# The write of the router weights, issued on ScalarE's DMA queue instead of SyncE's

## The chip, the core and the metric

The kernel runs on one core of a Trainium2 chip. The metric is the device time of one execution in microseconds; the kernel before took 3912.41 us, the median of three runs (3896.12 to 3922.23).

The names of the engines in the profile are PE (TensorE's matmuls), PEld (TensorE's weight loads), DVE (VectorE), ACT (ScalarE), POOL (GpSimd) and SP (SyncE, which here only issues DMAs). A "q" behind a name (SPq, ACTq) means the engine's sequencer, which waits, branches and issues DMAs.

## What is computed

The reference is one layer of a hybrid encoder on 1024 prompt tokens and 8 x 16 sample tokens, 1152 tokens in all, with width 1024: a mixer sublayer (banded attention beside a gated linear recurrence) and a PEER sublayer with 8 retrieval heads over 128 x 128 experts of one neuron each. The change lies on the way from the heads' choices to the weights of the experts:

```python
def peer_tokens(xt, wq, keys1, keys2, expert_u, expert_v):
    q = (xt @ wq).reshape(t, PEER_HEADS, 2, HALF_KEY)
    s1 = jnp.einsum('thd,hnd->thn', q[:, :, 0], keys1)
    s2 = jnp.einsum('thd,hnd->thn', q[:, :, 1], keys2)
    v1, i1 = lax.top_k(s1, TOPK_HALF)
    v2, i2 = lax.top_k(s2, TOPK_HALF)
    ...
    top_s, pos = lax.top_k(cand_s, TOPK)
    e_idx = jnp.take_along_axis(cand_i, pos, axis=-1)
    g = jax.nn.softmax(top_s, axis=-1)
    act = jax.nn.gelu(jnp.einsum('thkd,td->thk', expert_u[e_idx], xt))
    return jnp.einsum('thk,thkd->td', (g * act), expert_v[e_idx])
```

Each token has 8 x 16 chosen experts with a weight g each. As a matrix over all 16384 experts, g is nearly empty.

## The kernel before

The 1152 tokens are nine blocks of 128, in three groups of three. The mixer and the router run group by group. The experts are then computed in two ways. Four blocks (`GATHER`) fetch the chosen rows of `peer_u` and `peer_v` by indirect DMA on GpSimd's queue, and VectorE multiplies them (lines L915, L942, L963); this goes on beside everything else from about 700 us to the end. Five blocks (`DENSE`) are computed against all experts on TensorE at the end, from about 2060 us on, and need g as a full matrix `G_d` in DRAM, 128 x 128 experts by 640 tokens.

`build_g` makes that matrix, 32 tokens at a time, so 4 times a block and 20 times in all. One part of 8 tokens makes one-hot tiles on VectorE, 16 matmuls into two PSUM tiles `pg` (`products`, L1013 and L1014), and two ScalarE copies from `pg` into `st` (L1016). `st` holds 32 tokens, 128 partitions x 128 x 32 words, and its pool has one buffer, so the first L1016 of the next 32 tokens has to wait until the write of the last 32 has landed. The write is the line that changes, L1018: 2 MB from `st` to `G_d` in 8192 pieces of 256 bytes (64 words).

These parts are not a stage of their own. They stand in a list, `fill`, that `tick` empties a part at a time between the steps of the next group's mixer and router (L395 to L730), so the 20 writes fall between 980 and 2042 us: eight of them while the second group is in its attention, its output projections and its query projections, twelve while the third is. The instructions are then put in order, engine by engine, by a scheduler when the kernel is built; that order is fixed and every engine works through its own in order.

Before the change all weight loads and the write stand on one queue, SP's: `raw` (L149, a weight tile of 512 KB), `lo` (L159, the stored low part of a weight, 512 KB, read back instead of computed again), and smaller ones. ScalarE turns `raw` into `hi` (L158), and each projection is three matmuls a step (L170 to L172) with `hi` and `lo`. ScalarE's own queue carries other writes: keys and values (L484), router scores `s_d` (L730), and the rows of the residual and the normed tokens (L700, L708).

A built program counts the landing of its DMAs on eight semaphores, which the DMAs of both hardware queues take in turn: the DMA that is eighth after another takes the same one, and its issue waits until that other one has landed. With 8 semaphores and 20 writes, some of the DMAs that wait for a `G_d` write in this way are on ScalarE's queue.

Of the kernel before, what the change touches and what calls it, by code (L numbers as in the profile page):

```python
# [59 lines left out]
GCH = 2  # L60
# [10 lines left out]
def kernel(ctx, tc, a):  # L71
    nc = tc.nc
# [679 lines left out]
    def make_tables(b):  # L752
        if b in pending:
            pending.pop(b)()

    def table_parts(tab):
        h = tab.bitcast(F16)
        return h[:, 0:128], h[:, 128:256], tab[:, 128:192].bitcast(BF16), h[:, 384:512], h[:, 512:640]
# [213 lines left out]
    G_d = dr_p.tile([128, 128 // GCH, NCH, GCH, 32], F32, name="G_d")  # L972

    def build_g(gp, b):

        n0 = 4 * DENSE.index(b)
        st = {}

        def part(c, tb):
            def go():  # L980
                if c == 0 and tb == 0:
                    make_tables(b)
                    st["t"] = gp["st"].tile([128, 320], F32, name="tab")
                    nc.sync.dma_start(st["t"], tab_d[b])
                if tb == 0:
                    st["s"] = gp["st"].tile([128, 128, 32], F32, name="st")
                i1, i2, pw, hi, lo = table_parts(st["t"])
                sg = st["s"]
                t = c * 32 + tb * OH_T

                def row(x):
                    return x[:, t:t + OH_T].rearrange("p (g t) -> p g t", t=2).unsqueeze(2).to_broadcast(
                        [128, OH_T // 2, 128, 2])

                ow = gp["oh"].tile([128, OH_T // 2, 128, 2], BF16, name="ow")
                oh = gp["oh"].tile([128, OH_T // 2, 128, 2], F16, name="oh1")
                ol = gp["oh"].tile([128, OH_T // 2, 128, 2], F16, name="oh2")
                V.tensor_tensor(ow, gp["iota"], row(i2), op=ALU.is_equal)
                V.tensor_tensor(ow, ow, row(pw), op=ALU.mult)
                V.tensor_tensor(oh, gp["iota"], row(i1), op=ALU.is_equal)  # L1000
                V.tensor_tensor(ol, oh, row(lo), op=ALU.mult)
                V.tensor_tensor(oh, oh, row(hi), op=ALU.mult)
                later.append(lambda: products(c, tb, ow, oh, ol, sg))
                if len(later) > 1:
                    later.popleft()()
            return go

        def products(c, tb, ow, oh, ol, sg):
            for j0 in range(0, OH_T, 4):
                pg = ps_p.tile([128, 4, 128], F32, name="pg", tag="pp")  # L1010
                for j in range(4):
                    g, e = divmod(j0 + j, 2)
                    T.matmul(pg[:, j, :], ow[:, g, :, e], oh[:, g, :, e], start=True, stop=False)  # L1013
                    T.matmul(pg[:, j, :], ow[:, g, :, e], ol[:, g, :, e], start=False, stop=True)  # L1014
                t = tb * OH_T + j0
                S.activation(sg[:, :, t:t + 4].rearrange("p i t -> p t i"), pg, ACTF.Copy, scale=2.0 ** -13)  # L1016
            if tb == 32 // OH_T - 1:
                nc.sync.dma_start(G_d[:, :, n0 + c], sg.rearrange("p (a i) t -> p a i t", i=GCH))  # L1018

        later = deque()  # L1020
        return [part(c, tb) for c in range(4) for tb in range(32 // OH_T)] + [lambda: later.popleft()()]
# [290 lines left out]
```

## Time and profile before

| | |
|---|---|
| three runs | 3896.12, 3912.41, 3922.23 us |
| the profiled execution | 3894.32 us, of it 3892.5 us span |
| mean granted TensorE clock | 0.968 of full speed |
| TensorE busy | 3629.8 us, 93% of the span |
| VectorE, ScalarE, GpSimd busy | 78%, 42%, 37% |

The profile is of one execution, 18 us faster than the median of the runs. An engine's busy time leaves out what its sequencer does: waits and the issue of DMAs. The granted clock is a share of TensorE's full speed, 2.4 GHz; 0.5 is its lower level, 1.2 GHz. "idle before <- X" behind an instruction says how long its engine had nothing to run and what ended that.

### The profile page before, as it was taken

The numbers are of one execution on the slowest core, as the hardware profiler recorded it, in microseconds if no ns is written. First come the engines' busy times: TensorE is split into PE (matmuls) and PEld (weight loads), VectorE is DVE, ScalarE is ACT, GpSimd is POOL, SyncE is SP. The second block draws the span as 40 slices with busy tenths as digits, with TensorE's granted clock in tenths as the row PEclk, the third lists the DMA queues.
The fourth block names the chain that finished last, engine by engine and source line by source line (L and its number), as shares of the span: only waits on it lengthen the run. The fifth ranks groups of instructions, "written<-read, shape, count | busy, mean of one in ns | idle before, by whom it ended". The sixth has DMA issues, their size and how long they took to land.

```text
span 3892.5 us, 59562 instructions
## 1 busy us (share of the span) xinstructions
PE 3629.8 (93%) x21775; PEld 3258.9 (84%) x21775; DVE 3049.4 (78%) x6332; ACT 1624.7 (42%) x2699; POOL 1429.2 (37%) x1094
## 2 busy tenths in 40 slices
PE   8998899899988889988788989999999999999998
PEld 7877799877778887777778878999999999999997
DVE  8433357968766588987669999998888998888997
ACT  7554346656644664666443222222222222222222
POOL 0000000123212012322210666665675665775662
PEclk9999999999999999999889999999999999999999
DMA  7778887888999889899996999898998998998995
GB/s 256 252 247 300 287 295 276 301 315 281 284 358 349 300 299 315 298 290 284 334 337 216 345 326 342 320 347 332 359 339 310 346 347 326 336 349 324 342 343 206
DMA packets 558423, 1208.05 MB, mean 310 GB/s; under 512 B 205361, under 2 KB 281521, under 8 KB 558129
## 3 DMA queue, kind: packets, MB, share of 16 engines
q1 hardware_dynamic: 380560, 638.23, 47.3%
q0 software_dynamic: 147456, 536.94, 38.4%
q10 hardware_dynamic: 30112, 29.09, 2.2%
q8 instruction: 170, 2.79, 0.3%
q14 instruction: 125, 1.02, 0.1%
HBM read 1066.15 MB, written 137.94 MB: 309 GB/s over the span
## 4 chain that ended last, share of the span: by engine, by line
PE 61%; DVE 13%; DMA 10%; ACT 6%; issue 3%; POOL 0%; ACTq 0%; SPq 0%; DVEq 0%; POOLq 0%
PE S L1085 19%; PE pp L170 12%; PE pp L171 12%; PE pp L172 12%; DMA G_d<-st 4%; DVE row L942 3%; PE S L529 2%; ACT st L1016 2%; DMA row<-peer_u,ei 1%; PE pt L458 1%; PE pp L543 1%; ACT hi L158 1%; DVE x L963 1%; DMA lo<-lo_w_in 1%; DVE lo L137 1%
## 5 line engine op out<-in xcount | busy, mean ns | idle before, releaser
L915 POOL DMA_INDIRECT row<-peer_u,ei x512 | 715.2, 1397 | 1172.0 <-DVE row L942 508.6
L915 POOL DMA_INDIRECT row<-peer_v,ei x512 | 687.8, 1343 | 793.4 <-DVE x L963 543.0
L963 DVE SCALAR_TENSOR_TENSOR x<-row,q,x 128x1024 f32<-128x1024 f32 x512 | 655.0, 1279 | 21.3 <-DMA row<-peer_v,ei 12.5
L170 PE MATMUL pp<-xd,hi 128*128 128x320 f32 x2048 | 635.9, 310 | 16.4 <-ACT wf L1048 12.8
L942 DVE SCALAR_TENSOR_TENSOR row<-row,xt 128x1024 f32<-128x1024 f32 x512 | 613.2, 1218 | 42.7 <-DMA row<-peer_u,ei 41.1
L172 PE MATMUL pp<-xd,lo 128*128 128x320 f32 x2048 | 634.3, 310 | 4.5 <-DVE lo L137 4.5
L171 PE MATMUL pp<-xd,hi 128*128 128x320 f32 x2048 | 634.7, 310 | 0.0
L170 PE MATMUL pp<-xn,hi 128*128 128x384 f32 x1344 | 480.2, 358 | 13.9 <-ACT hi L158 6.9
L171 PE MATMUL pp<-xn,hi 128*128 128x384 f32 x1344 | 463.2, 345 | 0.5 <-DVE xn L137 0.5
L172 PE MATMUL pp<-xn,lo 128*128 128x384 f32 x1344 | 461.1, 344 | 0.9 <-DMA lo<-lo_w_in 0.9
L136 ACT CAST hi<-raw 128x1024 fp32r<-128x1024 f32 x223 | 234.0, 1050 | 447.0 <-PE pp L171 329.6
L170 PEld LDWEIGHTS pp<-xd,hi 128*128 128x128 f32 x2048 | 386.8, 189 | 26.0 <-ACT wf L1048 15.6
L137 DVE TENSOR_TENSOR lo<-raw,hi 128x1024 fp32r<-128x1024 f32 x223 | 272.3, 1222 | 171.1 <-ACT hi L136 151.0
L1085 PE MATMUL S<-vh,wh 128*128 128x512 f32 x1280 | 397.2, 392 | 5.2 <-DVE acc L1093 3.5
L1085 PE MATMUL S<-vl,wh 128*128 128x512 f32 x1280 | 396.0, 390 | 1.7 <-DVE vl L137 1.7
L1085 PE MATMUL S<-vh,wl 128*128 128x512 f32 x1280 | 390.1, 394 | 5.9 <-DVE wl L137 5.9
L171 PEld LDWEIGHTS pp<-xd,hi 128*128 128x128 f32 x2048 | 386.7, 189 | 7.1
L172 PEld LDWEIGHTS pp<-xd,lo 128*128 128x128 f32 x2048 | 386.6, 189 | 6.6 <-DVE lo L137 4.8
L158 ACT CAST hi<-raw 128x1024 fp32r<-128x1024 f32 x192 | 200.5, 1047 | 316.3 <-PE pp L171 215.8
L1048 ACT ACTIVATE wf<-pp 128x320 f32<-128x320 f32 x256 | 106.7, 434 | 524.7 <-PE pp L172 316.8
L170 PEld LDWEIGHTS pp<-xn,hi 128*128 128x128 f32 x1344 | 261.7, 195 | 38.3 <-ACT hi L158 9.7
L1085 PEld LDWEIGHTS S<-vh,wl 128*128 128x128 f32 x1280 | 242.2, 190 | 58.3 <-DVE wl L137 7.8
(296 smaller groups left out, 6824.7 us busy)
## 6 DMA issues: line engine op xcount, KB each, us to landing
raw<-w_in SPq DMA_DIRECT2D x168, 512.0 KB
raw<-peer_v SPq DMA_DIRECT2D x128, 512.0 KB
raw<-peer_ut SPq DMA_DIRECT2D x127, 512.0 KB
lo<-lo_w_in SPq DMA_DIRECT2D x112, 512.0 KB
G_d<-st SPq DMA_DIRECT2D x20, 2048.0 KB
gt<-G_d SPq DMA_DIRECT2D x64, 640.0 KB
lo_w_in<-lo SPq DMA_DIRECT2D x56, 512.0 KB
raw<-wq SPq DMA_DIRECT2D x48, 512.0 KB
```

The lines of the kernel that those rows point to most:

```text
L136: S.copy(r32(hi), src)
L137: ins = V.tensor_tensor(r32(lo), src, hi, op=ALU.subtract)
L158: S.copy(r32(hi), raw)
L170: T.matmul(out, r32(lh), r32(rh), start=first, stop=False)
L171: T.matmul(out, r32(lh), r32(rl), start=False, stop=False)
L172: T.matmul(out, r32(ll), r32(rh), start=False, stop=last)
L529: T.matmul(s[:, m, 0:nh], st["q"][r0:r0 + 64, i * 128:(i + 1) * 128], kf[r0:r0 + 64, ko + m * nh:ko + (m + 1) * nh], start=True, stop=True)
L915: P.indirect_dma_start(out=t, out_offset=None, in_=table, in_offset=bass.IndirectOffsetOnAxis(ap=ei[:, j:j + 1], axis=0))
L942: V.scalar_tensor_tensor(u, u, 1.0, xt, op0=ALU.mult, op1=ALU.mult, accum_out=hh[:, j:j + 1])
L963: V.scalar_tensor_tensor(x2, v, q[:, j:j + 1], x2, op0=ALU.mult, op1=ALU.add)
L1048: S.activation(w[:, c1], ps, ACTF.Gelu_apprx_tanh)
L1085: T.matmul(po[:, m, :], r32(l[:, c1]), r32(r[:, m * 512:m * 512 + 512]), start=(n == 0 and q == 0 and (c == 0 or not held)), stop=(n == EC ...
```

## The change

The write of the router weights is issued by ScalarE instead of SyncE, at the end of `products`:

```diff
             if tb == 32 // OH_T - 1:
-                nc.sync.dma_start(G_d[:, :, n0 + c], sg.rearrange("p (a i) t -> p a i t", i=GCH))
+                nc.scalar.dma_start(G_d[:, :, n0 + c], sg.rearrange("p (a i) t -> p a i t", i=GCH))
```

The orders of PE, DVE and POOL are the same before and after; SP's loses its 20 rows of L1018 and ACT's gains them, and nothing else moves.

On SP, in the query projections of the second group (the sixth write, issued at 1185.71 us in the trace; `lo_wq` is the stored low part of a query weight, `x` a block of the next group's input):

```order
 L159 DMA lo<-lo_wq_5598 128x1024
 L149 DMA raw<-wq 128x1024
-L1018 DMA G_d<-st 8192x1x64
 L159 DMA lo<-lo_wq_5633 128x1024
 L218 DMA x<-x 128x1024
```

The loads behind the write move up by one place.

On ACT, the same write (`st` is the tile that is written, `pq` a copy of a finished query projection):

```order
 L1016 ACTIVATE st<-pg 128x4x128
 L158 CAST hi<-raw 128x1024
+L1018 DMA G_d<-st 8192x1x64
 L719 COPY pq<-pp 128x384
 L158 CAST hi<-raw 128x1024
```

The write stands one instruction behind the last copy into `st`, and compute instructions follow it.

On ACT, in the query projections of the third group (the eighteenth write, issued at 1962.15 us in the trace; `so` is a head's router scores, `s_d` where they are written):

```order
 L120 ACTIVATE rms<-rs_m 128x1
 L729 COPY so<-S 128x768
+L1018 DMA G_d<-st 8192x1x64
 L730 DMA s_d_112<-so 128x768
 L158 CAST hi<-raw 128x1024
```

Here another DMA of ScalarE's comes right behind the write.

## Rows read from the trace of the kernel before

**Rows 1.** The page: the chain that ended last, shares by line.
```profile
PE S L1085 19%; PE pp L170 12%; PE pp L171 12%; PE pp L172 12%; DMA G_d<-st 4%; DVE row L942 3%; PE S L529 2%; ACT st L1016 2%; DMA row<-peer_u,ei 1%; PE pt L458 1%; PE pp L543 1%; ACT hi L158 1%; DVE x L963 1%; DMA lo<-lo_w_in 1%; DVE lo L
```

**Rows 2.** Busy time by stretch; the last three: clock, DMA share, GB/s.
```profile
950.00:1330.00 380.00, 332.02 (x2173) 298.04 (x2174) 252.42 (x593) 199.93 (x322) 74.23 (x63) 0.93 0.96 322
...
1620.00:2060.00 440.00, 371.66 (x2628) 325.00 (x2627) 334.14 (x643) 248.91 (x396) 105.82 (x78) 0.93 0.96 308
```

**Rows 3.** Line L1018: ns least/median/most of an issue, first and last start.
```profile
L1018 SPq DMA_DIRECT2D G_d<-st x20: 524/525/907, 980.7 to 2041.2; - x20
```

**Rows 4.** The chain in order of time: first and last of nine writes (start, us).
```profile
980.73 16.21 DMA G_d<-st
...
2008.20 19.37 DMA G_d<-st
```

**Rows 5.** PE's waits, 950 to 2060 us: total, times, longest.
```profile
PE pp L170 <- ACT hi L158: 29.5, 16, 5.9
PE pg L1013 <- ACT st L1016: 20.7, 12, 5.5
PE pp L170 <- ACT st L1016: 17.0, 15, 9.3
...
PE pg L1013 <- ACT pq L719: 14.6, 6, 7.2
PE pt L458 <- ACT st L1016: 8.1, 8, 5.8
```

**Rows 6.** SP's timeline (start, us) behind the sixth write.
```profile
1185.71 0.53 SPq L1018 DMA_DIRECT2D G_d<-st  x1
1186.33 13.49 SPq L159 DMA_DIRECT2D lo<-lo_wq  x1
1199.91 0.38 SPq L218 DMA_DIRECT2D x<-x  x1
```

**Rows 7.** ACT's timeline, the end of the same write.
```profile
1195.86 0.80 ACT L729 COPY so<-S 128x768 f32<-128x768 f32 x1 [0.64 <-PE S L727]
1201.83 0.38 ACTq L730 DMA_DIRECT2D s_d<-so  x1
1202.26 1.88 ACT L1016 ACTIVATE st<-pg 128x512 f32<-128x512 f32 x2 [5.60 <-DMA G_d<-st]
```

**Rows 8.** ACT's timeline behind the eighteenth write.
```profile
1964.32 0.33 ACTq L730 DMA_DIRECT2D s_d<-so  x1
...
1982.66 0.33 ACTq L708 DMA_DIRECT2D xt_d<-sq  x1
1983.02 0.48 ACT L719 COPY pq<-pp 128x384 f32<-128x384 f32 x1 [10.76 <-DMA G_d<-st]
```

**Rows 9.** Packets by queue (q1 SP, q0 POOL), 1032 to 1036 us.
```profile
q1 hardware_dynamic: 4483, 1.15, 126.1%
```

**Rows 10.** The same, 1196 to 1198 us.
```profile
q0 software_dynamic: 202, 0.76, 92.9%
q1 hardware_dynamic: 203, 0.05, 11.4%
```

**Rows 11.** The same, 950 to 1330 us: packets, MB, share of 16 engines.
```profile
q1 hardware_dynamic: 88949, 81.08, 66.1%
```

**Rows 12.** All queues, 1202 to 1212 us, behind the sixth write.
```profile
DMA packets 1091, 3.45 MB, mean 345 GB/s; under 512 B 127, under 2 KB 252, under 8 KB 1090
```

**Rows 13.** Busy time by stretch as in rows 2, behind the sixth write.
```profile
1203.30:1205.20 1.90, 1.86 (x17) 1.85 (x17) 0.07 (x1) 1.66 (x2) 0.00 (x0) 0.50 0.94 326
1205.20:1208.20 3.00, 3.00 (x12) 3.00 (x11) 3.00 (x6) 1.16 (x2) 0.00 (x0) 0.52 1.02 398
1208.20:1213.20 5.00, 5.00 (x30) 5.00 (x30) 2.33 (x5) 2.17 (x5) 2.62 (x2) 1.00 0.86 300
```

**Rows 14.** ACT's timeline: two more DMA issues behind writes.
```profile
2010.73 0.33 ACTq L730 DMA_DIRECT2D s_d<-so  x1
...
2045.97 0.33 ACTq L730 DMA_DIRECT2D s_d<-so  x1
```

## The prediction

> **What bounds the kernel now.** I read the chain that ended last first. TensorE's matmuls lead it, but 4% is the transfer `G_d<-st` [rows 1], and 4% of 3892.5 us is 156 us. In order of time these are nine of the 20 writes, with 16.2 us for the first and 19.4 us for the last from issue to release [rows 4]. The reader is to see that the chain runs through a landing: someone waits for the write to be over, not for its issue.
>
> Next, who waits. In the two stretches in which the writes fall TensorE idles 380.0 - 332.0 = 48.0 us and 440.0 - 371.7 = 68.3 us [rows 2]. Its waits between 950 and 2060 us name ScalarE [rows 5]: 20.7 + 17.0 + 8.1 = 45.8 us for `st` (L1016), 14.6 us for `pq`, 29.5 us for `hi`. The first two go back to a landing. Behind the sixth write ScalarE is done with `so` at 1196.66, but its next DMA, `s_d`, gets out only at 1201.83, and the copy into `st` follows after 5.60 us of idleness "<- DMA G_d<-st" [rows 7]. `s_d` is the eighth DMA behind the write and shares its semaphore, and the one `st` buffer is not free either. Behind the eighteenth write `xt_d` and `pq` wait 10.76 us in the same way [rows 8]. So 45.8 + 14.6 = 60.4 us of TensorE's idleness hang on the landing of writes, and at most 29.5 us, the waits for `hi`, on late weight loads.
>
> Last, the queue itself. Behind the write the next issue on SP is held: the load `lo` takes 13.49 us to issue, where the one after it takes 0.38 [rows 6]. It gets out at 1199.82, 14.1 us behind the write's issue. 18 of the 20 writes hold SP in this way. The other queue is not held: 2.2 us behind the eighteenth write ScalarE issues `s_d` in 0.33 us [rows 8]. The hold belongs to the queue that carries the write.
>
> **The loads that are freed.** The change takes 13 us or so of hold off SP up to 20 times. The cover is the prefetch: three to four weight tiles are loaded ahead, and the waits that could be late loads sum to 29.5 us [rows 5], spread over 1110 us, of which the holds are about 20 x 13 = 260. Late loads also show just behind a hold, so I put 12 of the 29.5 us on them. Bounds: 0 and -29.5 us. I take **-12 us**.
>
> **The landing of the write.** The write now starts beside the loads, not in front of them. Alone it runs at 4483 packets in 4 us, so its 8192 take 7.3 us [rows 9]. Beside the gathers of GpSimd's queue it gets 203 packets in 2 us while they get 202 [rows 10]: one packet of 256 bytes for one of 4 KB, a tenth of its pace. Every microsecond in which another queue moves large packets delays the write by about 0.9 us. Before, the hold kept the loads out of that window. SP moved 81.08 MB in the first stretch [rows 11], less 8 writes of 2.10 MB leaves 64.3 MB, or 123 loads of 0.524 MB in 380 us, 0.32 a microsecond; in the 16 us of a write that is 5 loads, of which one or two got through before. At the 345 GB/s of the stretch behind the hold, where loads were alone [rows 12], a load takes 1.5 us. So 3.5 more loads put the landing 5 us later in the projections; in attention, with about a third less to load, 2 us. More than seven loads can't go ahead, since the eighth DMA waits for the write. With 3 us as the mean, at the nine writes of the chain, that is 27 us, since TensorE's wait follows ScalarE's nearly one for one (5.60 us [rows 7] against the 5.5 us that is the longest wait of its kind [rows 5]). Bounds: +65 us if 13 writes land 5 us later; -20 us if the write lands 2 us earlier at ten places because nothing is queued ahead of it on ScalarE's ring. I take **+27 us**.
>
> **The hold moves to ScalarE.** The next DMA on the write's queue is held, and on ScalarE's queue a held issue stops all of ScalarE, since the compute instructions stand behind it in the same order. Where the next ScalarE DMA is far off, as behind the sixth write, where compute comes next and `s_d` 16 us later [rows 7], this costs nothing. At seven writes it is near: in the trace 0.3 us behind its new place at the eighteenth [rows 8], 2.5 us behind the nineteenth (2010.73 against 2008.20) and 4.8 us behind the last (2045.97 against 2041.2) [rows 3, 4, 14], and between 1.6 and 10 us at four more. A hold that ends 13.5 us behind the issue leaves 13, 11 and 9 us there, and about 8 on average at the others: 64 us of a stopped ScalarE. Queued behind are `hi`, `pq` and the attention's exponentials; TensorE waits for those. It has one projection ahead of it as cover each time (24 matmuls, 3.9 us by the kernel's constant `PROJ_US`), and at the eighteenth write it waited before as well, so I count half. Bounds: 0, if an issue on ScalarE isn't held, and +64. The nearest row is SP's own 13.49 us [rows 6], which speaks for the hold. I take **+32 us**.
>
> **The issue.** 20 issues of 0.525 us [rows 3] move to ScalarE, 10.5 us. ScalarE is busy about half of these stretches [rows 2], so half is on the path: **+5 us**, bounds 0 and +10.5.
>
> **The clock.** After the 5.5 us in which TensorE waits behind the sixth write its granted clock is 0.50 to 0.52 for 4.9 us, its lower level of 1.2 GHz, then 1.00 again [rows 13]. Such a wait costs 2.4 us more than itself. Three more of that length: **+8 us**, bounds -10 (four gone) and +15.
>
> The sum: -12 + 27 + 32 + 5 + 8 = **+60 us**. Against the profiled execution, 3894.3 us (3892.5 of span and 1.8 around it), that is 3954 us. The median of the runs lies 18 us above that execution, so against it I predict 3912 + 60 = **3972 us**. The sum's own range, with part of each bound, is +25 to +118 us: 3937 to 4030.
>
> **Rivals.**
>
> *The hold stays behind; only the landing counts.* If ScalarE's issue is not held, 32 us and most of the clock's share go: -12 + 27 + 5 + 2 = +22, 3934 us. For it: ScalarE's DMAs never show a long issue here [rows 8, 14]. Against: none of them stood behind a write of 8192 packets on its own queue.
>
> *Nothing changes.* The DMA engines are busy 0.96 of both stretches [rows 2]; if they are the limit, the loads and the write take the same time in whichever order, and what the loads gain the write loses: 3912 us. The Trainium skill, "DMA: Bandwidth & Descriptors", section "Issuing engines are not separate DMA queues", says this: DMAs from any engine run on the same 16 DMA engines and interleave, and issuing from several saves only the sequencer's time. By that rule the bandwidth gives nothing, which the trace bears out. Against no change: the landing and ScalarE's order matter here, not the total of bytes.
>
> *Faster.* The price is the hold of SP in front of the weight loads, the place every projection whose `lo` stands right behind a write [rows 6]. If late loads make all of the 29.5 us and the write lands 2 us earlier (-20), the clock gives 10 back and the issue is hidden, it is -29.5 - 20 - 10 = -60: 3852 us. It decides for the change if fewer than two extra loads meet a write and the seven near DMAs are not held. With half of it, 3882 us, it is still no change that can be told.
>
> *All holds reach TensorE.* Upper bounds together, 0 + 65 + 64 + 10.5 + 15 = +154: 4067 us. It would need TensorE without cover, as behind the sixth write, where its idleness began one microsecond after ScalarE stopped.
>
> **How the numbers follow.** I give the sum 0.58, the first rival 0.14, nothing 0.11, faster 0.08 and the upper bounds 0.09. Runs of this kernel lie between 3896 and 3922, so a change under about 1%, 39 us, can't be told from none. Slower by over 1% (above 3951): 0.50 of the 0.58, and 0.09, makes 0.59. Within 1%: the 0.08 left of the sum, 0.14, 0.11 and 0.03 of the faster case, 0.36. Faster by over 1%: 0.05. A range from 3895 to 4030 leaves out 0.06 below and some 0.09 above.
>
> **What would show it.** In the trace after: no issue on SP over 3 us between 980 and 2060 us, against 13.49; at the seven places an ACTq issue of 5 to 13 us; issue to landing of `G_d` at 18 to 24 us, not 16; TensorE's waits for `st`, `pq`, `hi`, `so` and the exponentials between 950 and 2060 us some 50 us longer in sum; and nothing changed after 2060 us but the start. I am wrong if ScalarE's issues stay at 0.33 us, and if landings come earlier.

## The result, and the profile after

The change made the kernel slower: 4032.19 us median against 3904.73 us (six runs each), a ratio of 1.0318 with a 95% interval of 1.0292 to 1.0345, which is 127 us. The profiled execution has a span of 4034.5 us, 142 us above the one before. The forecast was slower by 60 us, with a range that ended at 4030, 2 us short of this median: the direction and the two mechanisms were right, the size was half.

First the line that was moved, as its own view shows it (least, median, most of an issue in ns; who waited for it in us and times; issue to landing):

```profile
L1018 ACTq DMA_DIRECT2D G_d<-st x20: 520/521/587, 982.2 to 2174.3; - x20
...
  ACT st L1016: 101.8, 12
...
DMA to landing us min/median/max: 16.2/19.9/26.0
```

The issue costs what it cost on SP [rows 3]. But the writes land after 19.9 us in the median and 26.0 at most, where two of the chain's nine took 16.2 and 19.4 [rows 4]. Counted in the packets of both traces, a write's last packet starts 15.9 us behind its issue in the mean of the 20 before and 20.5 after. ScalarE's copies into `st` wait 101.8 us for landings; the same view of the kernel before has:

```profile
  ACT st L1016: 31.8, 9
```

SP's timeline behind the sixth write, issued on ScalarE's queue at 1218.59:

```profile
1219.45 0.33 SPq L218 DMA_DIRECT2D x<-x  x1
1222.18 0.33 SPq L159 DMA_DIRECT2D lo<-lo_wq  x1
1223.08 0.63 SPq L225 DMA_DIRECT2D gain<-norm_mix  x1
1226.88 0.33 SPq L159 DMA_DIRECT2D lo<-lo_wq  x1
```

Nothing holds the loads any more (0.33 to 0.63 us an issue, against 13.49 [rows 6]). The price stands on ScalarE, at the end of the same write:

```profile
1228.81 0.80 ACT L729 COPY so<-S 128x768 f32<-128x768 f32 x1 [0.68 <-PE S L727]
1241.56 0.34 ACTq L730 DMA_DIRECT2D s_d<-so  x1
1241.95 1.93 ACT L1016 ACTIVATE st<-pg 128x512 f32<-128x512 f32 x2 [12.34 <-DMA G_d<-st]
```

The same three instructions as in [rows 7], with 12.34 us of idleness where there were 5.60. TensorE's view of this end, and the clock in the 3 us after it (stretch, PE busy, ..., granted clock, DMA share, GB/s):

```profile
1243.03 0.27 PE L1013 MATMUL pg<-oh,ow 128*128 128x128 f16 x1 [12.27 <-ACT st L1016]
```
```profile
1243.00:1246.00 3.00, 2.98 (x20) 2.92 (x20) 1.13 (x2) 2.81 (x3) 0.00 (x0) 0.50 0.13 52
```

TensorE starts again at its lower level of 1.2 GHz, as behind the shorter wait before [rows 13].

What the change costs TensorE shows between the issue of the first write and that of the last, where it has the same 5963 matmuls in both kernels; first before, then after:

```profile
980.73:2041.22 1060.49, 925.65 (x5963) 818.78 (x5964) 794.84 (x2037) 589.27 (x965) 231.11 (x192) 0.94 0.94 314
982.25:2174.29 1192.04, 949.53 (x5963) 838.63 (x5964) 795.14 (x2037) 590.08 (x965) 228.83 (x192) 0.88 0.84 280
```

This stretch holds 131.5 of the 142 us. TensorE's idleness in it rises from 134.8 to 242.5 us, by 107.7, and the same matmuls take 23.9 us longer at a mean clock of 0.88 instead of 0.94. The DMA engines are less busy than before, 0.84 against 0.94: they are not what became short.

The second price is the hold on ScalarE's own queue. Behind the nineteenth write:

```profile
2129.54 0.52 ACTq L1018 DMA_DIRECT2D G_d<-st  x1
2130.39 0.80 ACT L729 COPY so<-S 128x768 f32<-128x768 f32 x1 [0.89 <-PE S L727]
2132.49 13.99 ACTq L730 DMA_DIRECT2D s_d<-so  x1
2146.52 1.04 ACT L158 CAST hi<-raw 128x1024 fp32r<-128x1024 f32 x1 [15.32 <-issue]
```
```profile
2147.99 0.69 PE L170 MATMUL pp<-xt,hi 128*128 128x384 f32 x1 [13.31 <-ACT pq L719]
```

The issue of `s_d`, 0.33 us before [rows 14], takes 13.99, the conversion of the next weight stands behind it, and TensorE idles 13.31 us. A view that names the waiter and the releaser says "issue" here, time in which ScalarE waited for nothing the profile shows; the ACTq row above it is the cause. Eight issues look like this, from 3.25 us (`v_all`, behind the ninth write) to 13.99, 81.8 us in sum.

Who waits, over both prices (TensorE's waits from 950 to 2200 us, to be read beside [rows 5]):

```profile
PE pg L1013 <- ACT st L1016: 65.8, 13, 14.0
PE pp L170 <- ACT hi L158: 40.2, 17, 14.3
PE pp L170 <- ACT st L1016: 31.6, 15, 16.7
PE S L529 <- ACT p L442: 25.9, 14, 8.6
PE pp L170 <- ACT pq L719: 22.1, 3, 13.3
PE pt L458 <- ACT pT L459: 11.8, 5, 9.2
PE pt L458 <- ACT st L1016: 9.6, 8, 7.4
```

The waits for `st` rise from 45.8 to 107.0 us, while the waits of L1013 for `pq`, 14.6 us before, fall to 3.4. `hi`, `p`, `pq` of the projections and `pT` are work that stands behind a held issue; where the eight near writes alone are moved (below), their waits rise as well and those for `st` don't.

Why the writes land later, in packets by queue during the sixth write, from issue to last packet. Before, 1185.7 to 1201.7 us (q1 is SP with the write on it, q0 GpSimd's gathers):

```profile
q1 hardware_dynamic: 8270, 2.35, 68.2%
q0 software_dynamic: 597, 2.15, 35.4%
```

After, 1218.6 to 1241.5 us (q10 is ScalarE's queue with the write, q1 the loads), and below it two microseconds inside, 1228 to 1230:

```profile
q10 hardware_dynamic: 8208, 2.10, 40.3%
q1 hardware_dynamic: 1014, 3.30, 36.4%
q0 software_dynamic: 602, 2.17, 25.5%
```
```profile
q0 software_dynamic: 111, 0.40, 50.1%
q1 hardware_dynamic: 102, 0.38, 47.5%
q10 hardware_dynamic: 111, 0.03, 6.2%
```

Beside the gathers, which are the same, 3.30 MB of loads now pass during the write where 2.35 - 2.10 = 0.25 did. While all three queues have work, they move about as many packets as one another, 111, 102 and 111, but the write's packet has 256 bytes and the others' 4 KB. With 3.05 MB, 5.8 loads, more beside it the write takes 6.9 us longer. Over all 20 writes, counted in the same way, SP's queue moves 2.61 MB beside a write where it moved 0.90, 3.3 loads more. The Trainium skill, "DMA: Bandwidth & Descriptors", section "Queues, rings and completion order", says that each DMA engine goes round the queues that have work, a packet at a time; the trace agrees in these counts, with one piece of 256 bytes for a packet of this queue, where the page calls some 9 to 17 descriptors in a packet typical.

### The profile page after: what moved, and what is told of

It is laid out like the page before. It is cut to its first block, busy times and chain, and to the rows that moved or that the text cites. A ratio compares the mean times of both kernels' runs of the same rounds, so it can differ in the third digit from the quotient of the medians.

```text
span 4034.5 us, 59557 instructions
## 1 busy us (share of the span) xinstructions
PE 3657.2 (91%) x21775; PEld 3283.5 (81%) x21775; DVE 3048.8 (76%) x6332; ACT 1625.5 (40%) x2699; POOL 1413.5 (35%) x1094
## 3 DMA queue, kind: packets, MB, share of 16 engines
q8 instruction: 170, 2.79, 0.3%
## 4 chain that ended last, share of the span: by engine, by line
PE 44%; DVE 9%; DMA 5%; ACT 3%; issue 1%; ACTq 1%; POOL 0%; SPq 0%; DVEq 0%; POOLq 0%
PE S L1085 18%; PE pp L170 8%; PE pp L171 8%; PE pp L172 8%; DMA G_d<-st 3%; DVE row L942 2%; ACT st L1016 1%; ACTq L730 1%; DVE x L963 1%; DMA row<-peer_u,ei 1%; PE S L529 1%; DVE lo L137 0%; DVE vl L137 0%; ACT hi L158 0%; DVE acc L1093 0%
## 5 line engine op out<-in xcount | busy, mean ns | idle before, releaser
L915 POOL DMA_INDIRECT row<-peer_u,ei x512 | 699.0, 1365 | 1250.0 <-DVE row L942 566.2
L170 PE MATMUL pp<-xn,hi 128*128 128x384 f32 x1344 | 486.1, 362 | 22.2 <-ACT st L1016 10.6
L171 PE MATMUL pp<-xn,hi 128*128 128x384 f32 x1344 | 468.4, 349 | 0.8 <-DVE xn L137 0.8
## 6 DMA issues: line engine op xcount, KB each, us to landing
G_d<-st ACTq DMA_DIRECT2D x20, 2048.0 KB, 19.9
```

What stands on the lines that cost most here:

```text
L170: T.matmul(out, r32(lh), r32(rh), start=first, stop=False)
L171: T.matmul(out, r32(lh), r32(rl), start=False, stop=False)
L915: P.indirect_dma_start(out=t, out_offset=None, in_=table, in_offset=bass.IndirectOffsetOnAxis(ap=ei[:, j:j + 1], axis=0))
```

## The experiments

The theory after the result: two places, each with half of the loss. **Landing**: the write goes beside the loads, lands some 5 us later, and the one `st` buffer and the DMAs of the same semaphore pass this on. **Hold**: the next DMA on ScalarE's queue stops ScalarE. The rivals: one of the two alone; or the traffic itself, loads and write disturbing each other whatever waits.

**The twelve far writes, and the eight near ones.** Far are the writes without another DMA of ScalarE's close behind them. One line each, against the changed kernel:

```diff
-                nc.scalar.dma_start(G_d[:, :, n0 + c], ...)
+                (nc.sync if n0 + c in (6, 7, 8, 10, 11, 17, 18, 19) else nc.scalar).dma_start(G_d[:, :, n0 + c], ...)
```

and the same with the two queues exchanged.

> Twelve of the 20 writes go on ScalarE's queue, those behind which no other DMA of ScalarE's comes within 13.5 us; the eight others (number 6, 7, 8, 10, 11, 17, 18, 19, counted from 0) are back on SyncE's queue. Every engine's order of compute is that of both kernels. Two-place theory: the loss has two halves, the later landing of the write and the hold of ScalarE by its next DMA. From one write's issue to the next the trace after is longer by 72 us in sum behind these twelve and by 68 us behind the eight, so this kernel should be 55 to 80 us slower than before, with ScalarE's issues all under 1 us and its waits for st some 60 us longer than before. Rival, the hold alone: with no hold left it is as fast as before, within 10 us. Rival, the landing alone: then the eight behind a hold lose by their landing too, and the twelve cost their share of 12 in 20, 76 us; the next kernel tells these two apart.

> The reverse: only the eight writes that have another ScalarE DMA close behind them go on ScalarE's queue, the twelve others stay on SyncE's. Two-place theory: 50 to 75 us slower than before, with eight ScalarE issues of 3 to 14 us, some 80 us in sum, and the twelve other landings as before. The hold alone: all of the loss, 115 to 135 us. The landing alone: ScalarE's long issues cost nothing that its wait for st would not have cost, and of these eight only three wait for st at once, so under 25 us.

Measured: the far writes alone 1.0180 (1.0147 to 1.0212), 3970.0 against 3901.7 us, 68 us; the near ones alone 1.0146 (1.0113 to 1.0178), 3960.1, 58 us. Together 126 of the 127 us, so the two parts add up and both rivals of one cause fall. The far kernel has no long issue on ScalarE; its waits for landings, in the view of L1018, are those of the changed kernel, and one for the eighteenth write, which is back on SP's queue:

```profile
  ACT st L1016: 101.7, 12
  ACT pq L719: 10.0, 1
```

The near kernel's is as before the change:

```profile
  ACT st L1016: 30.4, 9
```

Its eight issues are held from 3.13 to 13.43 us, 78.6 in sum. ScalarE's timeline behind one of them:

```profile
2062.30 13.04 ACTq L730 DMA_DIRECT2D s_d<-so  x1
2075.39 1.04 ACT L158 CAST hi<-raw 128x1024 fp32r<-128x1024 f32 x1 [13.58 <-issue]
```

The two kernels from the first write to the last, as above, the far writes first:

```profile
979.38:2116.58 1137.20, 941.20 (x5963) 831.71 (x5964) 795.46 (x2037) 589.99 (x965) 232.00 (x192) 0.90 0.88 293
978.66:2104.06 1125.40, 947.56 (x5963) 833.47 (x5964) 795.54 (x2037) 590.47 (x965) 231.35 (x192) 0.91 0.90 296
```

Against before, the far writes add 61.2 us of TensorE's idleness and 15.6 us of slower matmuls, the near ones 43.0 and 21.9; each is one profiled execution, so the parts add up only roughly, to 141.7 us against 131.5. This also answers the third rival, the traffic itself. TensorE's waits for `st` in the far kernel are

```profile
PE pg L1013 <- ACT st L1016: 65.0, 13, 14.5
PE pp L170 <- ACT st L1016: 31.0, 16, 16.7
PE pt L458 <- ACT st L1016: 11.5, 7, 8.6
```

107.5 us against 45.8 [rows 5], 61.7 more: as much as its idleness grew, so little of that is left for anything else.

**No ScalarE DMA behind the writes.** `nc.scalar` becomes `nc.sync` for `s_d`, `k_all`, `v_all`, `x2_d` and `xt_d`, while the 20 writes stay on ScalarE's queue. The order of compute changes in places.

> The changed kernel, the 20 writes on ScalarE's queue, with ScalarE's other writes (keys and values, router scores, residual and normed rows: 138 issues less five loads at the start) moved to SyncE's queue, so that no DMA of ScalarE's stands behind a write. 32-bit weights, one buffer for st. Two-place theory: no issue on ScalarE is held, all 20 writes land late: of the 58 us that the eight near writes cost most goes, so 65 to 100 us slower than before, nearer to the kernel with the twelve far writes alone; SyncE's loads may wait here and there behind writes that wait for ScalarE. Rival, that ScalarE's long issues were only where the landing showed: as slow as the changed kernel, 120 us and more.

Measured: 1.0221 (1.0203 to 1.0239), 87 us. No issue on ScalarE is longer than 0.67 us, and ScalarE's copies into `st` wait 119.2 us for landings, in 17 times instead of 12. The time is as the two-place theory expected, though with both the landing and the order of SP changed it is a weaker test than the two before.

**GpSimd's queue.** `nc.gpsimd.dma_start` in the same line.

> All 20 writes go on GpSimd's queue, beside the gathers' indirect DMAs. Neither SyncE's loads nor ScalarE's instructions stand behind them. Two-place theory: the hold is gone for both and the landing is late, as loads and gathers go beside the write; 60 to 100 us slower than before if GpSimd issues such a write as fast as the hardware queues do, more by as much as its issue takes, which no run has shown yet. The hold alone: as before or up to 30 us faster. The compute order differs in places from both kernels, since the scheduler weighs the queue.

Measured: 1.0006 (0.9989 to 1.0023), no change, so the expectation of the two places failed, and the number is the one that the hold alone would give, which the far writes have ruled out. The view of L1018 in this kernel:

```profile
L1018 POOL DMA_DIRECT2D G_d<-st x20: 2778/2787/2819, 979.7 to 2035.3; - x20
...
  ACT st L1016: 26.7, 10
...
DMA to landing us min/median/max: 15.0/17.4/19.4
```

I had overlooked two things. The gathers now stand on the write's own queue and no longer go beside it; and this queue moves the write in packets of 4096 bytes, not 256. The packets by queue, 950 to 2100 us:

```profile
q0 software_dynamic: 39354, 146.79, 39.3%
```

Before the change the same stretch has 28800 packets on q0, and the write adds 20 x 512 = 10240 of 4 KB, not 163840. (The Trainium skill, "DMA: Bandwidth & Descriptors", section "SWDGE vs HWDGE vs iDMA", gives packets of preferably up to 4096 bytes for the queue whose descriptors GpSimd writes; the trace agrees.) So the write's packets are as large as those of the loads; it lands at 17.4 us, of which 2.79 are the issue, and the waits for it are no longer than before. This run also sizes the other side of the change: here SP is freed of every hold as in the changed kernel (no issue over 2 us), at nearly the old landing, and the time does not move. What the freed loads give is within the interval, 4 us faster to 9 slower, together with the 20 longer issues on GpSimd and an order of compute that differs in places.

**A shorter write.** The weights in 16 bits (rounded to 11 bits), `GCH = 4` so that a piece stays 256 bytes, 4096 pieces, two buffers of `st` in the room of one, on SP's queue:

```diff
-GCH = 2
+GCH = 4
...
-                    st["s"] = gp["st"].tile([128, 128, 32], F32, name="st")
+                    st["s"] = gp["st"].tile([128, 128, 32], F16, name="st", bufs=2)
...
-            gt = dp["g"].tile([128, NCH, GCH, 32], F32, name="gt")
+            gt = dp["g"].tile([128, NCH, GCH, 32], F16, name="gt")
...
-    G_d = dr_p.tile([128, 128 // GCH, NCH, GCH, 32], F32, name="G_d")
+    G_d = dr_p.tile([128, 128 // GCH, NCH, GCH, 32], F16, name="G_d")
```

> The write stays on SyncE's queue. st, G_d and the tiles read back from it hold the weights in 16-bit floats, so the router weights are rounded to 11 bits (this changes part of the computation); four experts instead of two lie side by side, so that a piece stays 256 bytes and a write has 4096 pieces, 1 MB; st gets two buffers in the room of one. Two-place theory: the copies into st wait for no landing, the hold of SyncE halves to 7 us, the DMAs that share a semaphore with a write wait less; of the 60 us that TensorE waited on landings 35 to 60 come back, and part of the lower clock behind them: 40 to 75 us faster than before. Rival, the landing waits only hide other waits (late loads, ScalarE's own order): under 15 us faster.

Measured: 1.0322 (1.0289 to 1.0354), slower by as much as the change itself, although writes land in 7.8 us (median) and nothing waits for them. The group of the copies says why (out<-in, count | busy us, mean ns | idle before); first in the kernel before, then here:

```profile
L1016 ACT ACTIVATE st<-pg 128x512 f32<-128x512 f32 x160 | 160.2, 1106 | 46.3 <-DMA G_d<-st 31.8 <-PE pg L1014 13.0 <-issue 0.5
```
```profile
L1016 ACT ACTIVATE st<-pg 128x512 f16<-128x512 f32 x160 | 385.9, 2581 | 32.5 <-PE pg L1014 31.2 <-issue 1.2
```

The copy writes single words 32 words apart, and with 2-byte words that takes 2.3 times as long: 226 us more of ScalarE. So the run told nothing about the landing. Five more runs turn the order of the copy, so that four tokens lie in a row in its output:

```diff
-                S.activation(sg[:, :, t:t + 4].rearrange("p i t -> p t i"), pg, ACTF.Copy, scale=2.0 ** -13)
+                S.activation(sg[:, :, t:t + 4], pg.rearrange("p t i -> p i t"), ACTF.Copy, scale=2.0 ** -13)
```

> The kernel before (write on SyncE's queue, 32-bit st, one buffer), with one edit: ScalarE's copy from pg into st runs with the tokens innermost, so that it writes four words in a row and reads PSUM with a stride, where it wrote single words 128 bytes apart and read PSUM in a row. It is the control of the next two, and measures what the order of the copy costs by itself. If the stride of the output sets the copy's time, 160 copies of 1.11 us become shorter by some 0.3 us each and the kernel gains up to 30 us; if the stride of the PSUM read costs as much, no change; the landing, 16 us, and the waits for it should stay either way.

> As the kernel with 16-bit weights on SyncE's queue (rounded weights, 4096 pieces of 256 bytes, two buffers for st), with the copy's order turned as in the control. There the copy took 2.58 us instead of 1.11, 160 of them 235 us of ScalarE, and ate what the landing gave back. If single 16-bit words written with a stride were its cost, the copy comes back to about 1.1 us and the theory of the landing can be read: no wait of st for a write, and 30 to 70 us faster than before. If the copy stays near 2.6 us for any 16-bit output, 3 per cent slower as that kernel was.

> The kernel with 16-bit weights (rounded), tokens innermost, the write on SyncE's queue, but with one buffer for st. It parts the shorter write from the second buffer. If waiting for the landing is what counted, some 8 us of landing instead of 16 leave little to wait for, and it is within 15 us of its twin with two buffers; if the second buffer did it, it falls back towards the control in 32 bits, 40 us slower than its twin.

> The same kernel with the write on ScalarE's queue: the change under study, with half the packets and two buffers (rounded weights again). Two-place theory: the landing no longer matters, so only the hold is left, of about 7 us instead of 13 behind the writes that have a ScalarE DMA close behind them: 10 to 40 us slower than its twin on SyncE's queue. Rival, that the landing's share comes from loads that are disturbed by the write beside them and not from the wait for st: then the gap between the twins is over 50 us.

> The same kernel with the write on GpSimd's queue (rounded weights). There a write of 8192 pieces took 2.79 us to issue, moved in packets of 4096 bytes and held neither SyncE nor ScalarE. Two-place theory: no hold and no wait for the landing, so it is the fastest of the three, by 0 to 15 us against SyncE's, since the loads that are freed gave nothing that could be told with 32-bit weights. If it is over 20 us faster than SyncE's, the hold of SyncE did cost something that the landing hid.

| kernel, tokens innermost | ratio to before | 95% interval | median us |
|---|---|---|---|
| 32 bits, SP's queue | 0.9954 | 0.9934 to 0.9974 | 3876.8 |
| 16 bits, SP's queue, two buffers | 0.9849 | 0.9818 to 0.9880 | 3835.8 |
| 16 bits, SP's queue, one buffer | 0.9824 | 0.9806 to 0.9841 | 3827.4 |
| 16 bits, ScalarE's queue | 0.9924 | 0.9899 to 0.9950 | 3865.0 |
| 16 bits, GpSimd's queue | 0.9803 | 0.9763 to 0.9843 | 3819.0 |

The control and the 16-bit kernel on SP's queue, the group of the copies:

```profile
L1016 ACT ACTIVATE st<-pg 128x512 f32<-128x512 f32 x160 | 88.2, 600 | 53.7 <-DMA G_d<-st 31.6 <-PE pg L1014 12.9 <-issue 4.8
```
```profile
L1016 ACT ACTIVATE st<-pg 128x512 f16<-128x512 f32 x160 | 90.6, 599 | 33.8 <-PE pg L1014 27.1 <-PE pg L1013 6.2 <-PE pt L458 0.3
```

The copy takes 0.60 us with words of either size, and the control gains 17 us with its waits for landings unchanged, 31.6 us. The 16-bit kernel with two buffers is 41 us faster than the control (3835.8 against 3876.8), and no `st` waits for a landing in it. Not all of this need be the landing: the kernel's order of compute differs from the control's, and the dense stage reads half as much in `gt`. The traces show where the gain lies; first the control, then the 16-bit kernel:

```profile
980.57:2027.54 1046.97, 922.77 (x5960) 820.62 (x5961) 794.28 (x2033) 527.82 (x965) 229.43 (x191) 0.94 0.95 318
980.64:1954.33 973.69, 893.96 (x5938) 794.77 (x5939) 792.00 (x2025) 525.74 (x964) 220.00 (x189) 0.96 0.93 319
```

Between the first and the last write it is 73 us shorter, and from there to the end 1870.9 us against 1851.4, 19 longer. So the smaller reads of the dense stage are not the gain; what share the other order has, no run separates. With one buffer for `st` six waits for landings are left, 12.6 us, and the time is no longer than with two (0.9824 and 0.9849, again with different orders), so nothing shows a gain from the second buffer.

Between ScalarE's and SP's queue, in one order of compute, the 16-bit write costs 29 us (expected 10 to 40, over 50 for the rival of the traffic): five issues of 5.71 to 10.47 us on ScalarE, and one wait of 8.4 us for a landing. GpSimd's queue is the best of the three, 17 us ahead of SP's, two more than expected, with overlapping intervals and another order. At 0.9803 it beats both kernels, with rounded weights.

## Why the prediction was right in kind and half in size

Between the first and the last write the forecast had 52 us more of TensorE's idleness (-12 + 27 + 32 + 5) and 8 us of slower clock; the trace has 108 and 24. So each of three terms was too small: the landing, the hold and the clock.

*The freed loads, -12 us.* SP's holds did vanish, but they were worth nothing that can be told: the kernel on GpSimd's queue has none either and takes 1.0006 of the time before (with 16 bits, that queue was 17 us ahead of SP's, with overlapping intervals). That the prefetch covered them is likely, not shown.

*The landing, +27 us: mis-sized.* The far writes alone cost 68 us, 61 of them idleness of TensorE. The mechanism was as forecast, one small packet in turn with large ones, and so was the length in the projections: 5 us forecast, and in the traces 4.9 us, the mean of the eleven writes there. What failed was the 2 us for attention, where the last packets of nine writes (the first three, the ninth to the fourteenth) come 4.3 us later, and the choice of nine writes, those of the chain, as the places: those of the twelve far ones come 6.3 us later, and the waits for `st` grew from 31.8 us in nine to 101.8 us in twelve. The bound I gave beside it, 13 writes by 5 us, +65, was near. One reading in front of the sum was too high as well: of the 45.8 us in which TensorE waits for `st`, some 12 are the length of the copy, for in the control, with the shorter copy and the same waits for landings, they are 33.8. And in [rows 12] the loads are not quite alone: 0.39 of the 3.45 MB are on ScalarE's queue.

*The hold, +32 us: mis-sized.* The held issues sum to 81.8 us, not 64, at eight places, not seven (the eighth is the `v_all` of 3.25 us). The near writes alone cost 58 us. Taking half was nearly right in the sum, since 78.6 us of held issues brought 43.0 us of idleness, but not for the reason given: at the nineteenth write the projection that I counted as cover each time gave next to none, 13.31 us of idleness for 13.99.

*The clock, +8 us: mis-sized.* 24 us: behind more and longer waits more of TensorE's work is done at the lower level, and the mean clock from the first write to the last is 0.88 instead of 0.94. I had priced three more waits of 5.5 us.

*The issue, +5 us.* Not told apart: the issues of 0.52 us are in both halves.

*The rivals.* "The hold stays behind" fell with the eight long issues. "Nothing changes" fell too: the bytes are the same and the time is not, since order and waits changed. The Trainium skill, "DMA: Bandwidth & Descriptors", section "Issuing engines are not separate DMA queues", calls the sequencer time that another issuing engine saves usually small beside the DMA; here it isn't, with a held issue of 13.49 us on SP for a write of 16.0, and on ScalarE that time is compute. "Faster" had its price wrong: late loads were worth nothing that can be told. "All holds reach TensorE" came nearest, +154 against 127 us, in part by luck: its landing was right, but TensorE idled for 55% of the holds, not all, and the clock cost 24 us where it had 15.

What the profile was to show: no issue on SP over 3 us between 980 and 2060 us, which came; ACTq issues of 5 to 13 us at seven places, eight with 3.25 to 13.99; a landing of 18 to 24 us, 16.2 to 26.0; 50 us more of TensorE's waits, some 97 for the same five tiles, 61 of them for `st`; nothing changed behind the writes but the start, 9 us from the last write to the end.

## What to carry to other kernels

In this kernel a DMA of many small pieces had two prices apart from its bytes. It held the next DMA of its own queue for most of the time to its landing (14.1 of 16.0 us on SP, 16.9 of 20.1 on ScalarE). And on SP's and ScalarE's queues it got one small piece for each large packet of the others. So look for a queue whose next DMA is far away, or whose engine doesn't compute meanwhile; ask what large transfers will go beside the write there, if something waits for its landing; and try first whether it can be made shorter. And look at what the instructions around it write: turning one copy's loop so that it writes four words in a row gave 17 us for nothing.

## What was not expected of the hardware

- ScalarE's copy of 128 x 512 words from PSUM took 1.11 us when it wrote 4-byte words with a stride of 128 bytes, 2.58 us with 2-byte words at 64, and 0.60 us for either size with four words in a row, the stride being on the PSUM side.
- GpSimd's queue moved the same 8192 pieces of 256 bytes in packets of 4096 bytes, with an issue of 2.79 us (1.71 us for 4096 pieces), against 0.52 us and 163840 packets in all on the other two.
- Behind the nineteenth write ScalarE's next issue got out at 2146.48, 16.9 us behind the write's own issue; behind the sixth, SP's next issues took 0.33 to 0.63 us each. What was held is the next issue of the same queue, not of the other hardware queue.
